# Gate products and branch products of one branch, taken in turn instead of in groups of four

## The chip, the core and the metric

The kernel runs on one core of a Trainium2 chip. The metric is the device time of one execution in microseconds (us), the median of a few runs. TensorE (PE) multiplies matrices, VectorE (DVE) and ScalarE (ACT) do elementwise work, SyncE (SP) issues the large loads.

## What is computed

Two transformer blocks for 256 tokens of width 2048. The part that matters here is the merge of three branches in the first block:

```
p = h @ w_in + b_in
u, v, q, k, v_att, z_pool, gates = jnp.split(p, IN_SPLIT_POINTS, axis=-1)
y_sgu = spatial_gating(...)
y_moba = moba_attention(q, k, v_att)
y_pool = multiscale_pool(...)
g_sgu, g_moba, g_pool = jnp.split(jax.nn.sigmoid(gates), N_BRANCH, axis=-1)
merged = (g_sgu * (y_sgu @ w_sgu_out) + g_moba * (y_moba @ w_moba_out)
          + g_pool * (y_pool @ w_pool_out))
return merged @ w_out
```

Each gate is a product over 2048 input channels, each branch output one over 512. The attention has eight heads, and at 256 tokens each is plain causal attention with a distance term.

## The kernel before

Activations lie with channels on the partitions, so a tile of 128 output channels by 256 tokens is one accumulation in a PSUM bank (`pm`, four banks in rotation). All products are made from two parts of each number, high and low: `mm3` (L363 to L365) issues three matmuls for each 128 input channels. A **gate tile** has 16 such steps, 48 matmuls; a **branch tile** has 4, so 12 matmuls. In the attention, `pd` banks are used.

A weight arrives as one item of 1 MB in a `raw` buffer (load on SP, L222) and is split by `split_piece` in two halves: ScalarE rounds a half to `wh` (L249), VectorE subtracts to get `wl` (L250). There are four `wh` buffers; `wl` and `raw` share nine. One item of `w_in` is the weight of one gate tile; one item of `w_moba_out` serves four branch tiles. Between them items of `w_ada` are mixed in ("sprinkled"), which only VectorE works on (L588, a weighted sum for the modulation).

The program is a list of units. A unit issues its matmuls; then up to four times it advances the pending evictions one step and splits one piece, until the items `ahead` of its own are split. A unit of a branch tile splits at most one piece. The attention (`moba`, L991) is a background generator, moved on one step by each gate unit; whoever needs its result early runs it dry with `until`. Its heads pass scores (VectorE, L1018), exponentials (ScalarE, L1023, L1024), normalisation (VectorE, L1029 to L1031), transposes (TensorE, L1038), a copy (ScalarE, L1040) and products with the values (TensorE, L1049 to L1051); each second head ends with L1055, L411 and L412.

A gate tile is evicted by ScalarE (L850, a tanh). A branch tile is evicted by VectorE (L873), added to the merged tile (L876), and in the last branch split into the two parts that `w_out` reads (ScalarE L414, VectorE L415).

The last branch is `w_moba_out`. Before, its order is: gates 0 to 3, gates 4 to 7, branch tiles 0 to 3, gates 8 to 11, branch tiles 4 to 7, gates 12 to 15, branch tiles 8 to 15. Behind it follows `w_out` with 512-column matmuls (L395 to L397), four items of 24 matmuls for each quarter of the output, beginning with two `pm` banks.

Of the kernel before, what the change touches and what calls it, by code (L numbers as in the profile page):

```python
# [161 lines left out]
class Kernel:  # L162
# [448 lines left out]
    def sprinkle(self, n):  # L611

        self.nada += n
        while self.nada >= 1 and self.more:
            self.nada -= 1
            self.add_item(*self.more.pop(0))
# [212 lines left out]
    def block1_in(self):  # L829
        nc, ins = self.nc, self.ins  # L830
        H = lambda k: self.h[k]
        win = ins["w_in"]
        self.ysgu, self.ymoba, self.ypool = [], [], []
        sprinkle = self.sprinkle

        def tile_unit(idx, fn, pump=1):
            it = self.add_item(win[idx])

            def f(w):
                p = self.psm()  # L840
                for k in range(16):
                    self.mm3(p[:, :T], w, H, k, k == 0, k == 15)
                return fn(p)
            self.unit([it], f, pump=pump)
            sprinkle(self.rate)

        def gate(store, j, bidx):
            def fn(p):
                o = self.hp()[:, :T]
                nc.scalar.activation(o, p[:, :T], AF.Tanh, scale=0.5, bias=self.hb[:, bidx:bidx + 1])  # L850
                store[j] = o
                yield
            return fn


        self.X1 = {}

        def branch(name, ysrc, n4, tg, place):
            it = self.add_item(ins[name][n4])
            for jj in range(4):  # L860
                def f(w, jj=jj):
                    p = self.psm()
                    self.until(lambda: len(ysrc()) == 4)
                    for k in range(4):
                        self.mm3(p[:, :T], w, lambda k: ysrc()[k], k, k == 0, k == 3,
                                 cols=slice(jj * 128, jj * 128 + 128))
                    return ev(n4 * 4 + jj, p)

                def ev(n, p):
                    while tg[n] is None:  # L870
                        yield
                    t = tg[n]
                    nc.vector.scalar_tensor_tensor(t, t, 1.0, p[:, :T], op0=OP.add, op1=OP.mult)  # L873
                    yield
                    if place:
                        nc.vector.tensor_tensor(self.mg[n], self.mg[n], t, op=OP.add)  # L876
                    if place == 2:
                        yield from self.later(2)
                        xt = self.act_tile()
                        self.split_act(xt, self.mg[n], 0.5)  # L880
                        self.X1[n] = xt
                self.unit([it], f, pump=0.4, bg=False, pieces=1)
            sprinkle((0.2, 0.6, 0.4)[place])

        tm, tp = [None] * 16, [None] * 16

        def gates(store, base, n4, pump=1):
            for n in range(n4 * 4, n4 * 4 + 4):
                tile_unit(base + n, gate(store, n, 40 + base + n), pump)
        self.rate = 0.7  # L890
        gates(tp, 16, 0, 2)
        for n4 in range(4):
            if n4 == 2:
                gates(tp, 16, 1)
            branch("w_sgu_out", lambda: self.ysgu, n4, self.mg, 0)
        self.rate = 1
        for n4 in range(4):
            branch("w_pool_out", lambda: self.ypool, n4, tp, 1)
            if n4 < 2:
                gates(tp, 16, n4 + 2)  # L900
        gates(tm, 0, 0)
        for n4 in range(4):
            if n4 < 3:
                gates(tm, 0, n4 + 1)
            branch("w_moba_out", lambda: self.ymoba, n4, tm, 2)

    def sgu(self):
        nc, ins = self.nc, self.ins
# [1231 lines left out]
```

## Time and profile before

| | before |
|---|---|
| median of 3 runs | 2968.15 us (2967.96 to 2971.61) |
| the profiled execution | 2971.89 us, span 2969.8 us |
| granted TensorE clock, mean | 0.994 |
| TensorE matmul busy | 2913.5 us (98%) |
| VectorE busy | 2028.6 us (68%) |
| ScalarE busy | 1418.5 us (48%) |

A busy share is an average over the span; the stretch of the last branch runs from about 430 to 566 us. In a timeline row stand the start in us, the length in us, the engine, the line, the operation with its tiles, and in brackets the idle time of the engine just before, with what ended it. Matmuls overlap, so the distance of two starts tells the pace, not the length of one. The names of tiles are the program's: `wh` and `wl` weights, `act` split activations, `pt` the merged tiles, `hp` small tiles.

### The profile page before, as it was taken

How to read it: one execution, taken by the hardware profiler on the slowest of the kernel's cores; microseconds unless marked ns; L12 is line 12 of the kernel's file. 1: busy time of each engine (PE TensorE's matmuls, PEld its weight loads, DVE VectorE, ACT ScalarE, POOL GpSimd, SP SyncE). 2: the span in 40 equal slices, each digit the busy share in tenths (PEclk: the TensorE clock that was granted, in tenths of full speed). 3: DMA queues.
4: the chain of work that ended last, by engine and by line, in shares of the span. 5: the costliest groups of instructions: out<-in, count | busy, mean ns of one | idle time of the engine just before them, and what ended most of it. 6: DMA issues, size and time to landing. Idle time of an engine off the chain costs nothing.

```text
span 2969.8 us, 44949 instructions
## 1 busy us (share of the span) xinstructions
PE 2913.5 (98%) x18143; PEld 2591.5 (87%) x18143; DVE 2028.6 (68%) x3400; ACT 1418.5 (48%) x2282; POOL 56.9 (2%) x109
## 2 busy tenths in 40 slices
PE   6999999999999999999999999999999999999998
PEld 4999999878888888888899997799988888888887
DVE  7888888878779889676648845555645555555555
ACT  4545444456545556455444344444445444344344
POOL 0000000000000001000000000000000000000000
PEclk9999999999999999999999999999999999999999
DMA  9987778775567677656466773356645555555553
GB/s 360 350 310 279 271 290 335 294 271 175 205 244 263 217 283 258 209 184 213 166 214 199 235 234 107 115 171 242 224 165 184 184 193 187 188 186 183 198 181 131
DMA packets 127233, 660.58 MB, mean 222 GB/s; under 512 B 23009, under 2 KB 36065, under 8 KB 57393
## 3 DMA queue, kind: packets, MB, share of 16 engines
q1 hardware_dynamic: 86258, 603.30, 57.2%
q10 hardware_dynamic: 34464, 35.47, 3.7%
q0 software_dynamic: 6304, 18.95, 1.7%
q8 instruction: 143, 2.34, 0.3%
q14 instruction: 64, 0.52, 0.1%
HBM read 632.42 MB, written 25.23 MB: 221 GB/s over the span
## 4 chain that ended last, share of the span: by engine, by line
PE 90%; DVE 6%; ACT 2%; DMA 1%; issue 1%; SPq 0%; ACTq 0%; DVEq 0%
PE pm L377 22%; PE pm L379 11%; PE pm L363 9%; PE pm L364 9%; PE pm L365 9%; PE pm L395 8%; PE pm L397 8%; PE pm L396 8%; DVE wl L250 3%; ACT wh L249 1%; PE pd L1834 0%; DVE raw L588 0%; PE pd L1770 0%; DMA raw<-w_ada 0%; PE pd L509 0%
## 5 line engine op out<-in xcount | busy, mean ns | idle before, releaser
L250 DVE TENSOR_TENSOR wl<-raw,wh 128x1024 fp32r<-128x1024 f32 (+1 forms) x972 | 1134.7, 1196 | 403.4 <-ACT wh L249 401.1
L249 ACT ACTIVATE wh<-raw 128x1024 fp32r<-128x1024 f32 (+1 forms) x972 | 964.7, 1031 | 317.0 <-PE pm L396 116.9
L377 PE MATMUL pm<-act,wh 128*128 128x512 f32 x2816 | 992.9, 396 | 4.9 <-DVE act L781 3.0
L379 PE MATMUL pm<-act,wl 128*128 128x256 f32 x2816 | 792.0, 281 | 0.0
L363 PE MATMUL pm<-act,wh 128*128 128x256 f32 (+1 forms) x2656 | 756.5, 285 | 5.7 <-DVE hp L873 3.5
L364 PE MATMUL pm<-act,wh 128*128 128x256 f32 (+1 forms) x2656 | 753.2, 284 | 0.9 <-DVE act L781 0.3
L365 PE MATMUL pm<-act,wl 128*128 128x256 f32 (+1 forms) x2656 | 751.0, 283 | 1.7 <-DVE wl L250 1.7
L377 PEld LDWEIGHTS pm<-act,wh 128*128 128x128 f32 x2816 | 529.1, 188 | 127.3 <-DVE act L542 2.3
L379 PEld LDWEIGHTS pm<-act,wl 128*128 128x128 f32 x2816 | 531.5, 189 | 1.2 <-issue 0.7
L363 PEld LDWEIGHTS pm<-act,wh 128*128 128x128 f32 x2656 | 504.9, 190 | 14.3 <-DVE hp L873 4.6
L364 PEld LDWEIGHTS pm<-act,wh 128*128 128x128 f32 x2656 | 503.9, 190 | 2.4 <-DVE act L781 0.7
L365 PEld LDWEIGHTS pm<-act,wl 128*128 128x128 f32 x2656 | 502.0, 189 | 2.3 <-DVE wl L250 2.3
L395 PE MATMUL pm<-wh,act 128*128 128x512 f32 (+1 forms) x1072 | 428.4, 400 | 9.2 <-ACT act L779 5.9
L397 PE MATMUL pm<-wl,act 128*128 128x512 f32 (+1 forms) x1072 | 424.2, 396 | 0.0
L396 PE MATMUL pm<-wh,act 128*128 128x512 f32 (+1 forms) x1072 | 423.2, 395 | 0.5 <-DVE act L781 0.5
L395 PEld LDWEIGHTS pm<-wh,act 128*128 128x128 f32 (+1 forms) x1072 | 201.3, 188 | 60.7 <-ACT act L779 6.5
L396 PEld LDWEIGHTS pm<-wh,act 128*128 128x128 f32 (+1 forms) x1072 | 201.8, 188 | 49.4 <-DVE act L781 1.5
L397 PEld LDWEIGHTS pm<-wl,act 128*128 128x128 f32 (+1 forms) x1072 | 201.5, 188 | 48.9 <-DVE wl L250 0.4
L383 ACT ACTIVATE hp<-pm 128x256 f32<-128x256 f32 x176 | 67.2, 383 | 351.5 <-PE pm L379 351.1
L588 DVE SCALAR_TENSOR_TENSOR raw<-raw,cond 128x2048 f32<-128x2048 f32 x96 | 218.9, 2284 | 5.2 <-DMA raw<-w_ada 5.2
L384 DVE TENSOR_TENSOR hp<-hp,pm 128x256 f32<-128x256 f32 x176 | 73.5, 419 | 210.2 <-ACT hp L383 210.2
L2080 DVE TENSOR_TENSOR x<-pm,x 128x512 f32<-128x512 f32 x32 | 22.1, 692 | 91.7 <-PE pm L397 91.6
(333 smaller groups left out, 1737.2 us busy)
## 6 DMA issues: line engine op xcount, KB each, us to landing
raw<-w_ada SPq DMA_DIRECT2D x96, 1024.0 KB, 6.5
raw<-w_up SPq DMA_DIRECT2D x88, 1024.0 KB, 4.9
raw<-w_ff SPq DMA_DIRECT2D x88, 1024.0 KB, 4.8
raw<-w_in SPq DMA_DIRECT2D x81, 1024.0 KB, 5.1
raw<-w_st SPq DMA_DIRECT2D x37, 1024.0 KB, 6.3
raw<-w_out SPq DMA_DIRECT2D x32, 1024.0 KB, 5.4
raw<-w_down SPq DMA_DIRECT2D x32, 1024.0 KB, 4.9
raw<-w_fd SPq DMA_DIRECT2D x32, 1024.0 KB, 4.8
```

The costliest lines, as they stand in the source:

```text
L249: nc.scalar.activation(vh[:, ks], r[:, ks], AF.Copy)
L250: nc.vector.tensor_tensor(vl[:, ks], r[:, ks], vh[:, ks], op=OP.subtract)
L363: nc.tensor.matmul(o, wh[:, kw, c], x[:, 0, sl], start=start, stop=False, skip_group_check=True)
L364: nc.tensor.matmul(o, wh[:, kw, c], x[:, 1, sl], start=False, stop=False, skip_group_check=True)
L365: nc.tensor.matmul(o, wl[:, kw, c], x[:, 0, sl], start=False, stop=stop, skip_group_check=True)
L377: nc.tensor.matmul(p.rearrange("p (a t) -> p a t", a=2), wh[:, kw, c], x, start=start, stop=False, skip_group_check=True)
L379: nc.tensor.matmul(p[:, T:], wl[:, kw, c], x[:, 0], start=False, stop=stop, skip_group_check=True)
L384: self.nc.vector.tensor_tensor(o, o, p[:, :T], op=OP.add)
L395: nc.tensor.matmul(o, x[:, 0, tok], wh[:, kw], start=start, stop=False, skip_group_check=True)
L396: nc.tensor.matmul(o, x[:, 1, tok], wh[:, kw], start=False, stop=False, skip_group_check=True)
L397: nc.tensor.matmul(o, x[:, 0, tok], wl[:, kw], start=False, stop=stop, skip_group_check=True)
L588: self.nc.vector.scalar_tensor_tensor(o, o, 0.5, self.cond, op0=OP.mult, op1=OP.mult, accum_out=self.m(seg, n))
```

## The change

The last branch gets a helper `one(n)`, called after branch tile n, which puts gate tile n + 2 there. Gates 0 and 1 come first; then branch tile 0, gate 2, branch tile 1, gate 3 and so on to gate 15; branch tiles 14 and 15 are the last. For these units the number of items split ahead is two instead of three. The other two branches stay as they were.

```
-        def tile_unit(idx, fn, pump=1):
+        def tile_unit(idx, fn, pump=1, ahead=3):
...
-            self.unit([it], f, pump=pump)
+            self.unit([it], f, pump=pump, ahead=ahead)
...
-        def branch(name, ysrc, n4, tg, place):
+        def branch(name, ysrc, n4, tg, place, between=None):
...
-                self.unit([it], f, pump=0.4, bg=False, pieces=1)
+                self.unit([it], f, ahead=3 if between is None else 2, pump=0.4, bg=False, pieces=1)
+                if between is not None:
+                    between(n4 * 4 + jj)
...
-        gates(tm, 0, 0)
+        def one(n):
+            if n + 2 < 16:
+                tile_unit(n + 2, gate(tm, n + 2, 42 + n), ahead=2)
+        one(-2)
+        one(-1)
         for n4 in range(4):
-            if n4 < 3:
-                gates(tm, 0, n4 + 1)
-            branch("w_moba_out", lambda: self.ymoba, n4, tm, 2)
+            branch("w_moba_out", lambda: self.ymoba, n4, tm, 2, one)
```

The new code is five lines longer, so a line L991 of before is L996 after, and L1040 is L1045.

On TensorE, behind the second gate tile of this branch, there stood before the products of head 5, the transposes of head 6 (`pg572`), and then the third gate tile (`pm604`):

```order
L1049 MATMUL pd580_4524<-pg582_4532,pt74_350 64x128
L1050 MATMUL pd580_4524<-pg582_4532,pt74_350 64x128
L1051 MATMUL pd580_4524<-pg582_4532,pt75_351 64x128
L1038 MATMUL pd602_4712<-ident_71,pg572_4477 128x128 x3
L363 MATMUL pm604_4721<-act40_195,wh578_4519 128x256
L364 MATMUL pm604_4721<-act40_195,wh578_4519 128x256
L365 MATMUL pm604_4721<-act40_195,wl579_4520 128x256
```

Now the products of head 6 (`pg598` is the copy of its transposes), the transposes of head 7 (`pg588`) and its products follow at once, and then branch tile 0 (`pm599`):

```order
L1054 MATMUL pd580_4524<-pg582_4532,pt74_350 64x128
L1055 MATMUL pd580_4524<-pg582_4532,pt74_350 64x128
L1056 MATMUL pd580_4524<-pg582_4532,pt75_351 64x128
L1043 MATMUL pd597_4698<-ident_71,pg572_4477 128x128 x3
L1054 MATMUL pd600_4708<-pg598_4702,pt74_350 64x128
L1055 MATMUL pd600_4708<-pg598_4702,pt74_350 64x128
L1056 MATMUL pd600_4708<-pg598_4702,pt75_351 64x128
L1043 MATMUL pd601_4712<-ident_71,pg588_4623 128x128 x3
L1054 MATMUL pd600_4708<-pg602_4716,pt74_350 64x128
L1055 MATMUL pd600_4708<-pg602_4716,pt74_350 64x128
L1056 MATMUL pd600_4708<-pg602_4716,pt75_351 64x128
L363 MATMUL pm599_4707<-act529_4154,wh578_4519 128x256
```

The third gate tile, which stood between the heads, has moved behind branch tile 0.

On ScalarE, in the same branch, the evictions of gates 2 to 4 (`pm604`, `pm610`, `pm619`) and the splits between them stood before like this; `wh608` and `wh614` are the weights of gates 5 and 6:

```order
L850 ACTIVATE hp605_4770<-pm604_4721,hb_78 128x256
L249 ACTIVATE wh608_4777<-raw597_4696 128x1024 x2
L850 ACTIVATE hp611_4832<-pm610_4783,hb_78 128x256
L249 ACTIVATE wh614_4839<-raw607_4775 128x1024 x2
L1040 ACTIVATE pg618_4853<-pd617_4849 128x384
L850 ACTIVATE hp620_4904<-pm619_4855,hb_78 128x256
```

Now, at gates 8 to 10 (`pm662`, `pm670`, `pm678`): `wh666` is the branch weight of branch tiles 8 to 11, `wh673` the weight of gate 10 and `wh681` that of gate 11; L414 belongs to branch tiles:

```order
L850 ACTIVATE hp663_5294<-pm662_5245,hb_78 128x256
L249 ACTIVATE wh666_5301<-raw657_5219 128x1024 x2
L414 ACTIVATE act669_5322<-pt137_759 128x256
L850 ACTIVATE hp671_5374<-pm670_5325,hb_78 128x256
L249 ACTIVATE wh673_5378<-raw664_5296 128x1024 x2
L414 ACTIVATE act677_5402<-pt164_969 128x256
L850 ACTIVATE hp679_5454<-pm678_5405,hb_78 128x256
L249 ACTIVATE wh681_5458<-raw672_5376 128x1024 x2
```

The split of a gate's weight stood three gates before its use and now, at these places, stands behind the eviction of the gate just before.

On VectorE, the end of the branch stood before as evictions of neighbouring branch tiles (`pm715`, `pm718`, `pm723`) with pieces of `w_out` weights between them:

```order
L873 SCALAR_TENSOR_TENSOR hp658_5243<-hp658_5243,pm715_5767 128x256
L588 SCALAR_TENSOR_TENSOR raw711_5756,mod_74<-raw711_5756,cond10_97 128x2048
L876 TENSOR_TENSOR pt164_969<-pt164_969,hp658_5243 128x256
L415 SCALAR_TENSOR_TENSOR act717_5785<-pt164_969,act717_5785 128x256
L873 SCALAR_TENSOR_TENSOR hp664_5305<-hp664_5305,pm718_5788 128x256
L250 TENSOR_TENSOR wl721_5805<-raw712_5759,wh720_5804 128x1024
L876 TENSOR_TENSOR pt164_969<-pt164_969,hp664_5305 128x256
L415 SCALAR_TENSOR_TENSOR act722_5809<-pt164_969,act722_5809 128x256
L873 SCALAR_TENSOR_TENSOR hp670_5367<-hp670_5367,pm723_5812 128x256
```

Now the evictions of branch tiles 11 and 12 (`pm703`, `pm710`) have the splits for gates 14 and 15 (`wl709`, `wl717`) between them:

```order
L873 SCALAR_TENSOR_TENSOR hp690_5540<-hp690_5540,pm703_5635 128x256
L876 TENSOR_TENSOR pt165_970<-pt165_970,hp690_5540 128x256
L415 SCALAR_TENSOR_TENSOR act704_5650<-pt165_970,act704_5650 128x256
L250 TENSOR_TENSOR wl709_5707<-raw699_5624,wh708_5706 128x1024 x2
L873 SCALAR_TENSOR_TENSOR hp698_5622<-hp698_5622,pm710_5712 128x256
L588 SCALAR_TENSOR_TENSOR raw700_5627,mod_74<-raw700_5627,cond10_97 128x2048
L876 TENSOR_TENSOR pt170_1034<-pt170_1034,hp698_5622 128x256
L415 SCALAR_TENSOR_TENSOR act712_5730<-pt170_1034,act712_5730 128x256
L250 TENSOR_TENSOR wl717_5787<-raw707_5704,wh716_5786 128x1024 x2
```

Each eviction of a branch tile has moved to a place where one gate's weight is split before the next eviction.

## Rows read from the trace of the kernel before

**Rows 1.** Stretches: us, busy PE, PEld, DVE, ACT, POOL (count), clock, DMA, GB/s.
```profile
440.00:540.00 100.00, 100.00 (x837) 99.09 (x836) 86.11 (x99) 44.80 (x68) 0.00 (x0) 1.00 0.89 333
540.00:566.00 26.00, 20.48 (x123) 17.75 (x122) 20.16 (x39) 11.29 (x18) 0.00 (x0) 0.93 0.60 218
```

**Rows 2.** Waits of TensorE, 543 to 583 us: total us, times, longest.
```profile
PE pm L363 <- DVE hp L873: 3.5, 3, 1.3
PE pm L395 <- DVE hp L873: 2.0, 1, 2.0
```

**Rows 3.** Timeline of TensorE at the start of `w_out`: start, length, what.
```profile
555.88 0.40 PE L397 MATMUL pm<-wl,act 128*128 128x512 f32 x1
558.24 0.69 PE L395 MATMUL pm<-wh,act 128*128 128x512 f32 x1 [1.97 <-DVE hp L873]
558.73 0.63 PE L396 MATMUL pm<-wh,act 128*128 128x512 f32 x1
...
561.99 0.39 PE L395 MATMUL pm<-wh,act 128*128 128x512 f32 x1
```

**Rows 4.** Stretches around the longest wait, columns as in rows 1.
```profile
550.00:555.00 5.00, 3.14 (x24) 2.94 (x24) 3.81 (x9) 2.09 (x4) 0.00 (x0) 1.00 0.37 126
558.00:562.00 4.00, 3.76 (x10) 2.98 (x11) 2.93 (x6) 1.09 (x3) 0.00 (x0) 0.57 0.37 154
```

**Rows 5.** Timeline of TensorE behind gate 1 of the last branch.
```profile
444.51 0.43 PE L1049 MATMUL pd<-pg,pt 128*64 128x128 f32 x2
...
445.31 0.55 PE L1038 MATMUL pd<-ident,pg 128*128 128x128 f32 x3
445.61 0.36 PE L363 MATMUL pm<-act,wh 128*128 128x256 f32 x1
```

**Rows 6.** Timeline of ScalarE: exponentials to L850, attention output to transposes' copy.
```profile
445.37 0.40 ACT L1023 ACTIVATE pg<-pg,sm 128x128 f32<-128x128 f32 x1 [4.09 <-DVE sm L1022]
...
446.26 0.46 ACT L850 ACTIVATE hp<-pm,hb 128x256 f32<-128x256 f32 x1
...
448.51 0.37 ACT L1055 ACTIVATE hp<-pd 128x256 f32<-128x256 f32 x1
...
449.24 0.47 ACT L1040 ACTIVATE pg<-pd 128x384 f32<-128x384 f32 x1
```

**Rows 7.** Timeline of VectorE: a head's scores, a split, L412 with the normalisation.
```profile
443.94 0.54 DVE L1018 SCALAR_TENSOR_TENSOR pg<-dm,pd 128x384 f32<-128x384 f32 x1
...
445.24 2.28 DVE L588 SCALAR_TENSOR_TENSOR raw<-raw,cond 128x2048 f32<-128x2048 f32 x1
...
447.70 2.36 DVE L250 TENSOR_TENSOR wl<-raw,wh 128x1024 fp32r<-128x1024 f32 x2 [0.17 <-ACT wh L249]
449.98 0.42 DVE L412 TENSOR_TENSOR act<-hp,act 128x256 fp32r<-128x256 f32 x1
...
450.97 2.28 DVE L588 SCALAR_TENSOR_TENSOR raw<-raw,cond 128x2048 f32<-128x2048 f32 x1
```

**Rows 8.** Timelines of ScalarE and VectorE: a gate's eviction and a weight's split.
```profile
482.41 0.47 ACT L850 ACTIVATE hp<-pm,hb 128x256 f32<-128x256 f32 x1 [3.34 <-PE pm L365]
482.78 2.00 ACT L249 ACTIVATE wh<-raw 128x1024 fp32r<-128x1024 f32 x2
...
483.87 2.36 DVE L250 TENSOR_TENSOR wl<-raw,wh 128x1024 fp32r<-128x1024 f32 x2 [1.14 <-ACT wh L249]
```

**Rows 9.** Timeline of VectorE: one branch tile's eviction, first and next instruction.
```profile
495.92 0.41 DVE L873 SCALAR_TENSOR_TENSOR hp<-hp,pm 128x256 f32<-128x256 f32 x1
...
497.62 2.28 DVE L588 SCALAR_TENSOR_TENSOR raw<-raw,cond 128x2048 f32<-128x2048 f32 x1
```

**Rows 10.** Timeline of VectorE: L597 to L601, first and next instruction.
```profile
564.16 0.15 DVE L597 TENSOR_TENSOR mod<-mod,vecs 128x4 f32<-128x4 f32 x1
...
565.34 2.29 DVE L588 SCALAR_TENSOR_TENSOR raw<-raw,cond 128x2048 f32<-128x2048 f32 x1
```

**Rows 11.** The page's groups: busy us, mean ns of one, idle before.
```profile
L365 PE MATMUL pm<-act,wl 128*128 128x256 f32 (+1 forms) x2656 | 751.0, 283 | 1.7 <-DVE wl L250 1.7
```

## The prediction

> **What bounds the kernel now.** I read the busy table by stretches first, then TensorE's waits, then the timelines of TensorE, ScalarE and VectorE around the waits. From 440 to 540 us TensorE is busy the whole 100 us at a granted clock of 1.00: 837 matmuls, so one starts each 0.119 us, a gate tile (48) takes 5.7 us and a branch tile (12) 1.43 us [rows 1]. VectorE is busy 86 of those 100 us, so it has little to spare. From 540 to 566 us TensorE is busy for only 20.48 of 26 us [rows 1]. Its waits there are four, all on line L873 of VectorE, which evicts branch tiles: three of branch matmuls (3.5 us) and one of the first `w_out` item (2.0 us) [rows 2]. Four PSUM banks rotate, so the fifth tile in a row waits until the first is evicted. Counted from one matmul's start to the next, with a small further gap of 0.2 us, the four cost 6.3 us (5.5 us of rows 2, and in each some 0.16 us of the matmul's own drain). Behind the longest (555.88 to 558.24 [rows 3]) the granted clock falls to 0.57 in 558 to 562 us, near the lower level of 1.2 GHz, where it was 1.00 before [rows 4]. The starts from 558.24 to 561.99 span nine matmuls in 3.75 us [rows 3]; nine at 0.23 us would take 2.1, so 1.7 us are lost. **6.3 + 1.7 = 8.0 us is all that this stretch can give back.**
>
> **The change, part by part.** No instruction is added or removed on TensorE, ScalarE or VectorE; the order and the places of the loads change.
>
> *Branch tiles apart.* Between two branch tiles now stands a gate tile of 5.7 us, and an eviction takes 1.7 us (L873, L876, ScalarE's L414, L415; 495.92 to 497.62 [rows 9]). All PSUM waits of rows 2 go, except that the last three branch tiles stand near the end with one gate tile among them, which four banks hold: -8.0 us, the clock's share included. The Trainium skill, page "Perfetto Trace Analysis", section "Optimizing Tensor Performance", says that independent groups of matmuls should rotate through PSUM banks so that the eviction of one overlaps the next group. By that rule alone the change would give those 8.0 us; no sentence below rests on it.
>
> *Attention is asked for earlier.* Branch tile 0 needs all eight heads of the attention, which runs in the background between gate tiles. It now stands after gate 1 instead of gate 7. The order of TensorE shows what that does: the products of heads 5, 6 and 7 follow each other with no gate tile between. I follow it from gate 1's end at 444.5 us [rows 5]. TensorE does head 5's products and head 6's transposes until 445.6. ScalarE must evict gate 1 (0.37), split gate 2's weight (1.9) and pass L1055 and L411 (0.73) before it copies head 6's transposes (0.47) [rows 6, 8]: 444.6 + 3.5 = 448.1, so TensorE idles 2.5 us. Head 6's products take 0.8 us [rows 5], to 448.9. Head 7's scores are early (1.3 us of VectorE, free at 439.5; the two exponentials 0.9 us of ScalarE) [rows 6, 7], but their normalisation stands behind VectorE's half of the same split (from 446.1, 2.28 us) and takes 1.0 us with L412 ahead of it [rows 7]: 449.4, idle 0.5. The copy of head 7's transposes on ScalarE then costs 0.8 us of idling and the last L1055, L411 and L412 some 0.3 us. Sum **+4.1 us**. Before, gate tiles hid all of this: rows 1 show no idle time there.
>
> *Gate weights come later.* Before, a weight was split three items ahead. Now the branch weight holds one of the four `wh` buffers for four tiles, the lead is two, and the next branch weight counts as one of them. The order of ScalarE shows that the split of a gate's weight then stands right behind the eviction (L850) of the gate just before it, for gates 3, 6, 7, 10, 11, 14 and 15. From that gate's last matmul the chain is 0.28 (its own time [rows 11]), 0.37 for L850, 1.09 to VectorE's half and 1.22 for the half that TensorE needs first [rows 8], with three hand-overs of 0.05 us (my estimate from the difference of starts): 3.1 us. TensorE has the last matmul's slot, a branch tile and two matmuls that need only the high part, 15 x 0.119 = 1.8 us. It idles 1.3 us. So for gates 3, 7, 11 and 15; for 10 and 14 the eviction of another branch tile stands ahead on ScalarE (0.3 more). 4 x 1.3 + 2 x 1.6 = **+8.4 us**.
> Gate 6 is worse: from the end of gate 4 VectorE has to do an eviction (1.7), two `w_ada` reductions (L588, 2 x 2.2 [rows 7, 9]), the next branch weight's split (2.28), L873 and L876 of branch tile 3 (0.9); then ScalarE L414 and L850 (0.7), and the split up to the first half (2.3 and a hand-over): 12.4 us. TensorE has branch 3, gate 5, branch 4 and two matmuls: 8.8. **+3.6 us.**
>
> *The first items of `w_out`.* After gate 15 the two last evictions (2 x 1.7) and L597 to L601 (1.2 [rows 10]) stand on VectorE between the two halves of the second `w_out` weight. From the start of the first weight's split: 2.28 + 2.2 + 1.14 + 3.4 + 1.2 + 1.22 = 11.4 us; TensorE has 1.3 us until its third matmul starts, and then 36 matmuls at 0.23 = 8.3: idle 1.8, and 0.6 at the first weight. **+2.4 us.**
>
> *The load queue.* The lead of loads also shrinks, but SP's transfers were issued two gate tiles ahead of the split in my walk through the order; DMA's share was 0.89 in 440 to 540 us [rows 1], and a slower TensorE asks for less per us. I take 0; if one weight lands late, the bound is one more wait like that of gate 6, +3.6 us.
>
> *The clock.* It fell after an idle stretch of 2.1 us [rows 3, 4], and not after those of 1.3 us in 550 to 555 us [rows 4]. The stalls in the attention (2.5 us at once) and at gate 6 (3.6 us) are longer than the first; a fall costs up to 1.7 us. None to two: I take one, weighted for its overlap with idling, **+1.4 us**; bounds 0 and 3.4.
>
> **Sum:** 4.1 + 8.4 + 3.6 + 2.4 + 1.4 = +19.9; minus 8.0: **+11.9 us**. The profiled execution took 2971.89 us, 3.7 us above the median of 2968.15; on the former the sum gives 2983.8, on the median, which I forecast, **2980 us** (+0.4%). What follows this stretch keeps TensorE busy (98% over the span), so the delay is carried to the end one to one. A walk of the same kind through the order of before gives 7.0 us for the four waits where the trace has 6.3, so terms of mine may be a tenth too high.
>
> **Rivals.**
> *Gain, 2960 us.* The PSUM waits go and the weights still come in time. It would need the split of gates 7, 10, 11, 14, 15 to be issued at least 1.3 us sooner against TensorE; above that point each gate costs nothing, and if the attention's 4.1 us were hidden as well, -8.0 is left. For it: VectorE idles 14 of 100 us [rows 1]. Against it: the order puts the split behind an eviction that cannot start before the gate ends, and no idle time of VectorE helps that. 0.06.
> *A wash, about 2970 us.* Hand-overs and halves overlap better than I reckon: gates at 0.6 us each (4.2), attention 3, gate 6 and `w_out` 1.5 each, no fall: +10.2 - 8.0 = +2. Against it: each term has its durations in rows. 0.13.
> *The clock swings, 2992 us.* Each of the seven late gates is followed by a stretch at the lower level: 7 x 1.7 = 11.9 more. Against it: the three waits of branch tiles, 3.5 us together [rows 2], left the granted clock at 1.00 in 550 to 555 us [rows 4]. 0.06. The Trainium skill, page "TensorE: Matmul & The Clock Gate", section "A second HAM failure mode: psum-queue depth-cycling", tells of short idle times between groups of matmuls that let the gate swing between its levels, so that throughput suffers; by it this rival would be the result, and rows 4 show the opposite so far.
> That the order does not change as said is excluded by the order of TensorE.
>
> **How the numbers follow.** The forecast, 0.75, has its own range of 2975 (the terms a tenth lower, no fall, gate 6 at half) to 2986 (two falls, one late load). With the wash 0.13, the gain 0.06 and the swing 0.06, the range 2972 to 2988 leaves out the gain, the swing and the lower half of the wash. Faster or slower by over 0.2% (5.9 us), about what a measurement of this kernel can tell from no change: the forecast lies above 2974.1 but for its lowest end, so slower 0.80, same 0.14, faster 0.06.
>
> **What would show it.** In the profile of the changed kernel: no wait on L873 behind branch tiles; TensorE waiting on ScalarE's copy (L1045, before L1040) and VectorE's L1035 near 446 to 451 us; waits of about 1.0 us on VectorE's L250 at the third matmul of gates 3, 7, 10, 11, 14, 15, spaced 8 us apart in pairs, with a longer one at gate 6; one wait in the second `w_out` item; a granted clock below 1 behind the longest of them. I am wrong if gate tiles start without waits, or if the loads of `w_in` rather than the splits are what they wait for.

## The result, and the profile after

| | before | after |
|---|---|---|
| median | 2968.15 us (5 runs, 2967.96 to 2971.61) | 2984.11 us (5 runs, 2982.72 to 2984.88) |
| the profiled execution | 2971.89 us, span 2969.8 us | 2984.01 us, span 2981.8 us |
| granted TensorE clock, mean | 0.994 | 0.993 |
| TensorE matmul busy | 2913.5 us | 2920.0 us |

The changed kernel is slower: ratio 1.0051, 95% interval 1.0038 to 1.0064. The two profiled executions differ by 12.0 us of span, the medians by 16.0. Before each reading below I name the view.

How much of it lies in the stretch that was edited can be read from two landmarks that both programs have: ScalarE's first eviction of a gate tile (L850), and TensorE's first matmul behind the first L605, two items into `w_out` (L605 is a small product that spreads a row of the modulation, from L597 to L601). First the kernel before, timelines of ScalarE and TensorE (start, length, what):

```profile
282.36 0.46 ACT L850 ACTIVATE hp<-pm,hb 128x256 f32<-128x256 f32 x1
...
570.68 0.79 PE L395 MATMUL pm<-wh,act 128*128 128x512 f32 x1
```

The same two of the changed kernel:

```profile
282.08 0.45 ACT L850 ACTIVATE hp<-pm,hb 128x256 f32<-128x256 f32 x1
...
583.25 0.80 PE L395 MATMUL pm<-wh,act 128*128 128x512 f32 x1
```

From one to the other it takes 288.3 us before and 301.2 after: **+12.9 us, which is the whole difference of the two spans (12.0 us) and 0.9 us more.** Below I call this the length of the stretch.

The changed kernel by stretches, columns as in [rows 1] and the first two windows the same ones:

```profile
440.00:540.00 100.00, 90.58 (x704) 86.78 (x703) 70.45 (x89) 38.80 (x59) 0.00 (x0) 0.97 0.71 265
540.00:566.00 26.00, 24.14 (x197) 23.33 (x196) 21.24 (x24) 8.13 (x12) 0.00 (x0) 1.00 0.84 319
...
450.00:454.00 4.00, 3.80 (x18) 3.47 (x19) 0.42 (x1) 0.95 (x3) 0.00 (x0) 0.57 0.52 221
...
487.00:491.00 4.00, 3.25 (x16) 3.12 (x15) 4.00 (x4) 0.51 (x1) 0.00 (x0) 0.60 0.76 270
...
525.00:565.00 40.00, 37.30 (x302) 36.08 (x302) 31.03 (x36) 15.41 (x22) 0.00 (x0) 1.00 0.79 299
```

Where TensorE was busy for all of 440 to 540 us, it now idles 9.4 of the 100, with 704 matmuls in place of 837. The granted clock falls twice, to near 1.2 GHz, in 450 to 454 and in 487 to 491 us; in 525 to 565 us, with three late gates (11, 14 and 15), it stays at 1.00.

Waits of TensorE in the changed kernel, 425 to 640 us (total us, times, longest):

```profile
PE pm L365 <- DVE wl L250: 5.5, 8, 0.8
PE pd L1054 <- ACT pg L1045: 2.9, 2, 2.3
PE pm L363 <- ACT wh L249: 2.3, 3, 1.8
PE pm L397 <- DVE wl L250: 1.4, 2, 1.1
PE pd L1043 <- DVE pg L1035: 0.3, 1, 0.3
PE pm L395 <- ACT wh L249: 0.2, 1, 0.2
```

The waits on L873 of [rows 2] are gone, all of them. In their place stand waits on the two halves of a weight (L249, L250) and on the attention (L1045, L1035). Of the eight on L365, seven are those of gates 3, 6, 7, 10, 11, 14 and 15, and one is in branch tile 4.

**The attention.** Timeline of TensorE before branch tile 0:

```profile
445.02 0.55 PE L1043 MATMUL pd<-ident,pg 128*128 128x128 f32 x3
447.84 0.43 PE L1054 MATMUL pd<-pg,pt 128*64 128x128 f32 x2 [2.28 <-ACT pg L1045]
...
449.01 0.61 PE L1043 MATMUL pd<-ident,pg 128*128 128x128 f32 x3 [0.31 <-DVE pg L1035]
450.20 0.68 PE L1054 MATMUL pd<-pg,pt 128*64 128x128 f32 x2 [0.58 <-ACT pg L1045]
```

ScalarE in the same place; the copy L1045 that TensorE wants at 445.3 stands last of these rows:

```profile
444.32 0.47 ACT L850 ACTIVATE hp<-pm,hb 128x256 f32<-128x256 f32 x1 [2.73 <-PE pm L365]
444.69 1.99 ACT L249 ACTIVATE wh<-raw 128x1024 fp32r<-128x1024 f32 x2
446.59 0.37 ACT L1060 ACTIVATE hp<-pd 128x256 f32<-128x256 f32 x1
446.99 0.42 ACT L411 ACTIVATE act<-hp 128x256 fp32r<-128x256 f32 x1
447.31 0.47 ACT L1045 ACTIVATE pg<-pd 128x384 f32<-128x384 f32 x1
```

**The late gates.** At gate 6 TensorE waits for the rounded half and then for the other one:

```profile
484.53 0.28 PE L365 MATMUL pm<-act,wl 128*128 128x256 f32 x1
486.62 0.39 PE L363 MATMUL pm<-act,wh 128*128 128x256 f32 x1 [1.81 <-ACT wh L249]
486.84 0.28 PE L364 MATMUL pm<-act,wh 128*128 128x256 f32 x1
487.88 0.58 PE L365 MATMUL pm<-act,wl 128*128 128x256 f32 x1 [0.75 <-DVE wl L250]
```

On ScalarE gate 6's split stands behind gate 5's eviction (485.17), and that behind branch tile 3's L414. VectorE held this up, with two L588 and the next branch weight's split ahead of the tile's L873 and L876:

```profile
484.84 0.42 ACT L414 ACTIVATE act<-pt 128x256 fp32r<-128x256 f32 x1 [5.72 <-DVE pt L876]
```

The cause of the others is plain on ScalarE and VectorE at gate 11. ScalarE:

```profile
526.57 0.47 ACT L850 ACTIVATE hp<-pm,hb 128x256 f32<-128x256 f32 x1 [1.33 <-PE pm L365]
526.94 2.94 ACT L249 ACTIVATE wh<-raw 128x1024 fp32r<-128x1024 f32 x3
```

VectorE, at the same time:

```profile
528.02 2.36 DVE L250 TENSOR_TENSOR wl<-raw,wh 128x1024 fp32r<-128x1024 f32 x2 [2.33 <-ACT wh L249]
```

ScalarE idles 1.33 us for gate 10's last matmul, then evicts, then splits; VectorE idles 2.33 us for the split. Both engines were idle just before, so by these rows it was the order that kept them from doing this weight earlier; the second experiment tests that.

### The profile page after: what moved, and what is told of

Read it like the earlier page. It is cut to its first block, busy times and chain, and to the rows that moved or that the text cites. A ratio compares the mean times of both kernels' runs of the same rounds, so it can differ in the third digit from the quotient of the medians.

```text
span 2981.8 us, 44945 instructions
## 1 busy us (share of the span) xinstructions
PE 2920.0 (98%) x18143; PEld 2594.1 (87%) x18143; DVE 2029.3 (68%) x3400; ACT 1417.5 (48%) x2282; POOL 56.9 (2%) x109
## 4 chain that ended last, share of the span: by engine, by line
PE 88%; DVE 8%; ACT 2%; DMA 1%; issue 1%; ACTq 0%; SPq 0%; DVEq 0%
PE pm L377 22%; PE pm L379 11%; PE pm L363 9%; PE pm L365 9%; PE pm L364 9%; PE pm L397 8%; PE pm L395 8%; PE pm L396 8%; DVE wl L250 3%; DVE raw L588 1%; ACT wh L249 1%; PE pd L1839 0%; PE pd L1775 0%; PE pm L527 0%; DMA raw<-w_ada 0%
## 5 line engine op out<-in xcount | busy, mean ns | idle before, releaser
L250 DVE TENSOR_TENSOR wl<-raw,wh 128x1024 fp32r<-128x1024 f32 (+1 forms) x972 | 1134.8, 1196 | 412.3 <-ACT wh L249 410.1
L249 ACT ACTIVATE wh<-raw 128x1024 fp32r<-128x1024 f32 (+1 forms) x972 | 964.0, 1031 | 325.4 <-PE pm L396 116.5
L377 PE MATMUL pm<-act,wh 128*128 128x512 f32 x2816 | 990.5, 396 | 4.9 <-DVE act L781 3.0
L379 PE MATMUL pm<-act,wl 128*128 128x256 f32 x2816 | 789.9, 281 | 0.0
L365 PE MATMUL pm<-act,wl 128*128 128x256 f32 (+1 forms) x2656 | 753.6, 284 | 6.9 <-DVE wl L250 6.8
L377 PEld LDWEIGHTS pm<-act,wh 128*128 128x128 f32 x2816 | 528.8, 188 | 127.0 <-DVE act L542 2.3
L379 PEld LDWEIGHTS pm<-act,wl 128*128 128x128 f32 x2816 | 531.0, 189 | 1.1 <-issue 0.7
L365 PEld LDWEIGHTS pm<-act,wl 128*128 128x128 f32 x2656 | 504.0, 190 | 9.4 <-DVE wl L250 9.4
L588 DVE SCALAR_TENSOR_TENSOR raw<-raw,cond 128x2048 f32<-128x2048 f32 x96 | 218.8, 2284 | 4.2 <-DMA raw<-w_ada 4.2
```

Of the source, the lines that this page charges most:

```text
L249: nc.scalar.activation(vh[:, ks], r[:, ks], AF.Copy)
L250: nc.vector.tensor_tensor(vl[:, ks], r[:, ks], vh[:, ks], op=OP.subtract)
L365: nc.tensor.matmul(o, wl[:, kw, c], x[:, 0, sl], start=False, stop=stop, skip_group_check=True)
L377: nc.tensor.matmul(p.rearrange("p (a t) -> p a t", a=2), wh[:, kw, c], x, start=start, stop=False, skip_group_check=True)
L379: nc.tensor.matmul(p[:, T:], wl[:, kw, c], x[:, 0], start=False, stop=stop, skip_group_check=True)
L588: self.nc.vector.scalar_tensor_tensor(o, o, 0.5, self.cond, op0=OP.mult, op1=OP.mult, accum_out=self.m(seg, n))
```

## The experiments

All medians are beside runs of the kernel before on the same chip; the 28 of the first group have a median of 2969.06 us. The last column is the length of the stretch in the one profiled execution, less the 288.3 us of before.

| | median us | ratio to before, 95% interval | stretch |
|---|---|---|---|
| after | 2984.11 | 1.0051, 1.0038 to 1.0064 | +12.9 |
| attention sooner | 2974.57 | 1.0017, 1.0008 to 1.0026 | +11.0 |
| pieces first | 2966.51 | 0.9988, 0.9979 to 0.9997 | -3.2 |
| both | 2960.39 | 0.9971, 0.9959 to 0.9982 | -3.9 |
| smaller groups | 2973.00 | 1.0010, 1.0001 to 1.0018 | -1.0 |
| lead of two alone | 2971.45 | 1.0007, 0.9998 to 1.0016 | +4.1 |
| before, attention sooner | 2968.69 | 1.0001, 0.9992 to 1.0010 | +1.0 |
| more banks | 2964.47 | 0.9985, 0.9976 to 0.9994 | -3.0 |
| both, `w_out` first | 2961.36 | 0.9972, 0.9962 to 0.9983 | -4.0 |
| banks, L605 later | 2957.84 | 0.9960, 0.9946 to 0.9974 | -7.3 |

(The two with more banks move L605, or end a fall of the clock behind it; their end landmark is the first matmul behind the second L605, a quarter of `w_out` later, and the length stands against 311.3 us of before.)

### The attention moved on sooner

```
-                gates(tp, 16, n4 + 2)
+                gates(tp, 16, n4 + 2, 2)
```

> The changed kernel, with the gate units of the pool branch ahead of it moving the attention on twice as fast, so that all heads are done before branch tile 0 asks for them. Theory (the attention's tail is asked for too early and costs its own 4.1 us, and about 1.7 us of lost clock behind it): the waits of TensorE on ScalarE's copy (L1045, 2.9 us in the changed kernel) and on VectorE's L1035 (0.3 us) near 446 to 451 us are gone, the granted clock stays at 1.00 there, the waits on L250 and L249 at the gates stay as they are, and the time falls by 4 to 6 us against the changed kernel, to about 2978 to 2980 us. Rival (the attention is short of VectorE or ScalarE time wherever it stands): the waits move some tens of us earlier into the pool branch and the time stays within 1.5 us of the changed kernel, 2982.5 to 2985.5.

Waits of TensorE, 425 to 640 us:

```profile
PE pm L365 <- DVE wl L250: 6.0, 9, 0.8
PE pm L363 <- ACT wh L249: 2.3, 3, 1.8
PE pm L397 <- DVE wl L250: 1.4, 2, 1.1
PE pm L395 <- ACT wh L249: 0.2, 1, 0.2
```

The waits on the attention and the first fall of the clock are gone, as the theory has it, and the rest stays. The median fell by 9.5 us, more than either view expected, but the stretch gave only 1.9 back: gate 2 now waits as well (a ninth wait on L250; the attention's wait had covered it), and the fall at gate 6 lasts twice as long (0.55 in 483 to 487 us, 0.60 in 487 to 491). Of the 3.8 us of waits and 1.7 of clock that went, gate 2 takes 1.2, and the longer fall 1.6 by the granted clock (0.9 by the distances of starts); the 0.8 to 1.5 us that remain were not followed to the end. One wait of 0.4 us on L873, in the pool branch, is new. So the attention's own price is confirmed by the waits that went, but alone it gives back half, because the next late thing stood right behind. The other 7.6 us came from outside the stretch, and their cause is open (see the end).

### The pieces of the next weight ahead of the evictions

```
+            if ahead == 2 and pieces == 4:
+                for s in range(4):
+                    if self.split < goal:
+                        self.split_piece()
+                pieces = 0
             for s in range(stages):
                 self.advance()
```

> The changed kernel, but a gate unit of the last branch issues the pieces of the next weight's split ahead of the eviction steps, so that ScalarE's split does not stand behind the tanh (L850) of the gate just before. Theory (a gate's weight is late by its place in ScalarE's queue, 8.4 us in all and 3.6 at gate 6): the waits on L250 (5.5 us, 8 times) and on L249 (2.3 us, 3 times) behind the gates go or fall under 1 us together, the clock falls once instead of twice, the attention's 3 us stay, and the time falls by 9 to 13 us, to 2971 to 2975 us. Rival (the weights are late because their loads land late, or because VectorE has no time left for the split): the waits stay, or become waits on a DMA, and the time stays within 3 us of the changed kernel, 2981 to 2987.

Five lines are added above the lines named here, so L370 is L365 of before, L1059 is L1049 and L855 is L850. Waits of TensorE, 425 to 640 us:

```profile
PE pd L1059 <- ACT pg L1050: 1.4, 2, 0.8
PE pm L402 <- DVE wl L250: 0.9, 1, 0.9
PE pm L370 <- DVE wl L250: 0.8, 1, 0.8
PE pm L400 <- ACT hp L855: 0.2, 1, 0.2
PE pm L368 <- ACT wh L249: 0.2, 1, 0.2
```

ScalarE at the same gate as above; the split now stands ahead of the eviction:

```profile
512.77 0.42 ACT L419 ACTIVATE act<-pt 128x256 fp32r<-128x256 f32 x1 [4.00 <-DVE pt L881]
513.10 2.94 ACT L249 ACTIVATE wh<-raw 128x1024 fp32r<-128x1024 f32 x3
515.95 0.45 ACT L855 ACTIVATE hp<-pm,hb 128x256 f32<-128x256 f32 x1
```

This decides the main question. With the same loads, the same work on each engine and the same lead of two, the 7.8 us of waits on L250 and L249 become 1.0, the clock does not fall in the stretch, and the time falls by 17.6 us, to just below the kernel before. The rival (loads, or VectorE's time) is out but for gate 6: the 1.0 us are all its own, since its split still stands behind L419 (L414 of before), which waits 5.72 us for VectorE as it did. It gave more than I expected since the attention's copies also stood behind a split (3.2 us of its waits become 1.4, and the fall behind them goes).

### Both edits

> Both edits of the changed kernel together: the attention moved on sooner, and the pieces of the next gate's weight ahead of the eviction steps. Theory (the terms add): only the waits of w_out's first items are left, about 1.5 to 2.5 us, no fall of the clock in 440 to 560 us, and the time is 2965 to 2969 us, at or a little below the kernel before. Rival (with the queues rearranged something that has no wait now becomes late, VectorE's evictions of branch tiles or the loads): the sum of the two single gains is not reached, and the time is over 2972 us.

Only three waits are left, 1.9 us together: 0.8 and 0.9 on L250 (gate 6 and `w_out`'s second item), 0.2 on L855. The time is 2960.39, under the range of the theory; its stretch of -3.9 us is what the theory needs, and more came from outside the stretch (3.4 us by the two profiled spans, 4.8 by the medians). So the order in turn, with its weights in time, is a gain over the groups, of which the stretch shows 3.9 us.

### Smaller groups, and lead of two alone

The kernel before, with eight, four, two and two gates ahead of its four groups of branch tiles:

```
-        gates(tm, 0, 0)
-        for n4 in range(4):
-            if n4 < 3:
-                gates(tm, 0, n4 + 1)
+        for g, n4 in ((8, 0), (4, 1), (2, 2), (2, 3)):
+            for n in range((0, 8, 12, 14)[n4], (0, 8, 12, 14)[n4] + g):
+                tile_unit(n, gate(tm, n, 40 + n))
             branch("w_moba_out", lambda: self.ymoba, n4, tm, 2)
```

> The kernel before, with its lead of three and its groups, but gates 12 to 15 not in one group: gates 0 to 7, branch tiles 0 to 3, gates 8 to 11, branch tiles 4 to 7, gates 12 and 13, branch tiles 8 to 11, gates 14 and 15, branch tiles 12 to 15, so that eight branch tiles never follow each other. Theory (the waits on L873 come from more branch tiles in a row than there are PSUM banks, and the gate weights are in time as long as the lead is three and the branch weight is held for a short time only): the three waits of branch tiles on L873 (3.5 us) are gone, the one at w_out (2.0 us) stays or shrinks, the clock stays at 1.00 if it shrinks, and the time falls by 4 to 8 us against the kernel before, to 2960 to 2964 us. Rival (the time is set by VectorE's work for the evictions and the splits, and the waits only change their names): the time stays within 2 us of 2968, with waits on L250 or at w_out of as many us as those that went.

Waits of TensorE, 425 to 640 us, and the window behind the longest:

```profile
PE pm L395 <- DVE hp L873: 4.1, 2, 3.0
PE pm L363 <- DVE hp L873: 0.6, 1, 0.6
```

```profile
552.00:558.00 6.00, 4.28 (x9) 2.99 (x10) 4.85 (x10) 1.78 (x3) 0.00 (x0) 0.50 0.86 347
```

My theory fell. The branch tiles' waits shrank from 3.5 us to 0.6, but that of `w_out` grew from 2.0 to 4.1 in two, and the clock stood at 0.50 for 6 us with them. The profiled execution was the fastest of eleven, so its stretch of -1.0 us may flatter the edit; the median is 4 us above before. Here a wait for a bank is also a wait for VectorE's queue: the smaller groups ask for the same evictions at the end.

The kernel before, with a lead of two items in place of three for the gates and branch tiles of the last branch, and its order as it was:

```
...
-                self.unit([it], f, pump=0.4, bg=False, pieces=1)
+                self.unit([it], f, ahead=2 if place == 2 else 3, pump=0.4, bg=False, pieces=1)
...
-                tile_unit(base + n, gate(store, n, 40 + base + n), pump)
+                tile_unit(base + n, gate(store, n, 40 + base + n), pump, 3 if base else 2)
```

Waits of TensorE, 425 to 640 us:

> The kernel before, with its groups, and only the other half of the change: the lead of the splits is two items instead of three for the gates and the branch tiles of the last branch. Theory (a lead of two is long enough as long as gate tiles stand in groups, since a gate tile is 5.7 us and a split 2.3; the weights come late only where an item that serves four tiles is interleaved and the split falls behind the eviction of the gate just before): no wait on L250 or L249 over 1 us in all, the waits on L873 as before, and the time within 3 us of the kernel before, 2966 to 2972 us. Rival (the lead alone makes the weights late): waits on L250 or L249 behind the gates of 5 to 12 us in all, and 2974 to 2984 us.

```profile
PE pm L363 <- DVE hp L873: 3.5, 3, 1.3
PE pm L395 <- DVE hp L873: 2.8, 1, 2.8
PE pm L365 <- DVE wl L250: 2.7, 2, 1.3
```

Between the two views: the lead alone makes two weights late, one behind each of two branch groups (2.7 us where I allowed 1, under the rival's 5 to 12), and `w_out` waits 0.8 us longer. The stretch grew by 4.1 us, the median by 2.4, which its interval cannot tell from nothing. Interleaving with a lead of three was not run; by my reading of the code the branch weight would hold one of the four `wh` buffers while ScalarE's next split waits for a buffer that is freed only behind it.

### The kernel before with the attention sooner

The edit of the first experiment on the kernel before.

> The kernel before, with the gate units of the pool branch moving the attention on twice as fast, as in the first experiment; nothing waited for the attention here. In that experiment the stretch of the last branch gave some 2 us back, and 7.5 us were gained far behind it, where the pairs of matmuls of L377 and L379 between 2300 and 2900 us started every 348.0 ns instead of 350.8. Theory (this far gain belongs to the earlier attention, by the places at which later tiles lie, and not to the waits of the last branch): the waits on L873 stay, the pairs start every 348 ns, and the time is 2963 to 2967 us. Rival (it was a chance of single executions, or it needs the interleaved order): the pairs keep 350.8 ns and the time stays within 2 us of 2969.

The waits on L873 are as they were and the median is unchanged, so the earlier attention is worth nothing by itself. The pairs of matmuls came every 349.6 ns, about half-way; the theory of the far gain is not borne out.

### More banks

```
-                    p = self.psm()
+                    p = self.pss() if place == 2 and jj % 2 else self.psm()
```

> The kernel before, order and lead as they were, but every second branch tile of the last branch takes its PSUM bank from pd instead of pm, so that eight tiles in a row find a bank free. Theory (the waits on L873 are for a PSUM bank and nothing else): the three waits of branch tiles (3.5 us) and the one of w_out (2.0 us) go, the granted clock stays at 1.00, and 8.0 us are given back: 2960 to 2963 us. Rival (VectorE is behind with the evictions and the splits, as the group of four smaller groups suggests, whose wait at w_out grew to 4.1 us): the same idle time comes back in w_out's first items, as waits on L873, on L415 or on L250 of together 4 to 7 us, and the time stays within 3 us of 2969.

Waits of TensorE, 425 to 640 us:

```profile
PE pd L605 <- DVE ad L601: 3.5, 1, 3.5
```

The instruction on VectorE that it waited for, which stands behind the last eviction:

```profile
564.44 0.87 DVE L601 TENSOR_SCALAR ad<-ident,mod 128x128 f32<-128x128 f32 x4
```

Both views hold in part. All four waits on L873 go with nothing but other banks, so it was the banks; and 3.5 us of idle time come back at the first instruction that needs VectorE to be through, with a fall of the clock behind it (0.64 in 565.4 to 569.4 us). 4.6 of 8.0 us are left.

### More banks, and L605 later

The edit above, and this one:

```
-        for _ in range(6):
+        for _ in range(18 if seg == 2 and q == 0 else 6):
             yield
         p = self.pss()
```

> The kernel with more banks, and one more edit: the matmul L605 of w_out's first quarter, which waited 3.5 us for L601 because VectorE still had eight evictions and splits ahead of it, is issued twelve steps of its unit later, in the next item. Theory (the 8.0 us of the PSUM waits are all there, and the kernel with more banks gave half back only because L605 was next in TensorE's queue): the wait on L601 goes, its fall of the clock goes too (1.7 us), a wait of about 1 us on L250 may come in w_out's fourth item, and the time falls by 4 to 5 us to 2959.5 to 2961 us, level with the interleaved order with both edits. Rival (VectorE is that far behind for every reader, so the idle time only moves to the next one): waits on L415 or L250 of 3 us or more in w_out's third and fourth items, and the time stays at 2963 to 2966 us.

Waits of TensorE, 425 to 640 us, and the stretch of [rows 1] in which it idled 5.5 us before:

```profile
PE pm L397 <- DVE wl L250: 0.8, 1, 0.8
```

```profile
540.00:566.00 26.00, 26.00 (x161) 23.34 (x161) 20.03 (x41) 11.13 (x17) 0.00 (x0) 1.00 0.74 280
```

The theory holds: one wait of 0.8 us is left, the clock stays at 1.00, and the stretch is 7.3 us shorter than before. At 2957.84 us this is the lowest median of all, without any change of the order of gates and branch tiles; its interval overlaps that of the kernel with both edits, but its stretch is 3.4 us shorter.

### Both edits, and w_out's weights first

In the kernel with both edits, the last two branch tiles may split up to four pieces ahead of their evictions.

```
-                self.unit([it], f, ahead=3 if between is None else 2, pump=0.4, bg=False, pieces=1)
+                self.unit([it], f, ahead=3 if between is None else 2, pump=0.4, bg=False,
+                          pieces=4 if between is not None and n4 * 4 + jj > 13 else 1)
```

> The kernel with both edits (attention sooner, split pieces ahead of the evictions in gate units), and the last two branch tiles too issue the pieces of w_out's weights ahead of their evictions, up to four pieces instead of one. Theory (the second w_out weight is late because its second half stands behind the two last evictions and L597 to L601): the wait on L250 in w_out's second item (0.9 us, 1.1 by starts) is gone, and the time is 2958 to 2960 us, 1 to 2 us under the kernel with both edits. Rival (the evictions that now stand later are what w_out needs next): a wait of 1 to 3 us on L420 or L878 in w_out's third or fourth item takes its place, 2960 to 2963 us.

Neither view, for the edit changed nothing that ran: from 440 to 600 us ScalarE and VectorE have the same instructions in the same order as without it. By the code, the goal of these two units counts two items from the branch weight, and those are the weights of gates 14 and 15, which are split by then. So the wait on L250 stays at 0.9 us, 2961.36 us is a second measurement of the kernel with both edits, and the theory was not tested. The second half still stands behind the two evictions and L602 to L606 (L597 to L601 of before).

## Why the prediction held, point by point

*The sum.* Forecast +11.9 us on the profile; the spans differ by 12.0. The terms, forecast and measured. A measured term is the sum of the distances of two starts in TensorE's timeline, less the usual slot (0.12 us for 256 columns, 0.23 for 512, 0.30 for the three transposes):

| term | forecast | measured |
|---|---|---|
| PSUM waits and their fall | -8.0 | -8.0 (no wait on L873 is left; the price is that of before) |
| attention | +4.1 | +3.8 (2.5, 0.4, 0.9) |
| gates 3, 7, 11, 15 | +5.2 | +4.6 (4 x 1.16) |
| gates 10, 14 | +3.2 | +2.7 (2 x 1.33) |
| gate 6 | +3.6 | +3.2 (2.9, and 0.3 at branch tile 4) |
| first items of `w_out` | +2.4 | +2.1 (0.50, 0.38, 1.26) |
| falls of the clock | +1.4 | +3.3 (0.43 x 4, 0.40 x 4) |
| load queue | 0 | 0 (no wait on a load) |
| sum | +11.9 | +11.7 |

The stretch is 12.9 us longer; 1.2 us lie in gaps too small to name. Each term of waiting was about a tenth too high, as the walk through the kernel before had said of itself: together 18.5 forecast, 16.4 measured. The term that failed is **the clock**: two falls, where I took one. They came where I had put them, behind the attention's stall and behind gate 6, and the reason that I gave (idle stretches longer than the 2.1 us one of [rows 3]) would, with the 2.5 and 3.6 us forecast there, have given both; I cut them to one, and that by 0.3, for overlap with idling. Gate 6's stall then came as 2.0 and 0.9 us with two matmuls between, so it was not one longer stretch, and the clock fell all the same. The window from 487 us shows an overlap with idling, but of 0.75 us only. The two errors, 2.1 us too high in the waits and 1.9 too low in the clock, nearly cancel; that the sum came out within 0.3 us is in part luck.

*The mechanism.* The second experiment shows it: a gate's weight is late by its place behind the eviction of the gate before in ScalarE's order. At gate 6 VectorE's two L588 come on top, as forecast; waits of 0.2 and 0.8 us are left there under the edit. The first shows that the attention stalled because it was asked for early.

*The rivals.* The gain at 2960 was put at 0.06, and on the order as it is that was right; its condition, a split issued at least 1.3 us sooner, is what the experiment with both edits gave, and the time came out as 2960.4; about half of that gain lies outside the stretch, though. The wash needed late gates of 0.6 us each; they took 1.16 and 1.33. The swing of the clock did not come: with three late gates in 525 to 565 us the granted clock stayed at 1.00. The Trainium skill, page "TensorE: Matmul & The Clock Gate", section "A second HAM failure mode: psum-queue depth-cycling", tells of a kernel whose short idle times between groups of matmuls made the clock swing. Here waits of 1.2 to 1.3 us, in pairs some 8 us apart, did not.

*The -8.0 us.* It was right as a term of this change, since branch tiles now stand apart, but "all that this stretch can give back" needed a second condition, which the prediction did not name: VectorE must be through by the next instruction that reads from it. With more banks alone 4.6 us came back, with L605 moved as well 11.1 in the median and 7.3 in the stretch. The Trainium skill's advice to rotate banks (page "Perfetto Trace Analysis", section "Optimizing Tensor Performance") is borne out by these two runs, once that reader is out of the way.

*The base.* I put the sum on the median of before; after's median came out 4 us higher. The profiled execution of before was one of its slower ones: among the 28 of the first group, the eleven with a granted clock of 0.993 or 0.994 took 2971.2 us in the mean, the seventeen with 0.995 or 0.996 took 2968.6. The five runs of after lie within 2.2 us, all at 0.992 or 0.993. Two falls in the stretch against one explain part of that. Why none of the five was as lucky elsewhere as most runs of before is open.

## What to carry to other kernels

In these traces ScalarE and VectorE took their instructions in the order of the program: ScalarE idled 1.33 us with gate 11's split next behind an eviction. So how many items ahead a weight is prepared counted less than which instruction stood before it. When tiles are interleaved, look for the preparation that now stands behind an eviction that cannot start before TensorE ends the tile in front; issuing it ahead of that eviction was worth 17.6 us here. And before reordering for a PSUM wait, see whether another bank is free: here two one-line edits gave the lowest median, with the order left alone.

## What the runs showed that I had not expected

Far behind the edit, TensorE's pace differs between these programs. Windows of 2300 to 2900 us, columns as in [rows 1], TensorE busy throughout; first the kernel before, then the one with the attention sooner:

```profile
2300.00:2900.00 600.00, 600.00 (x3170) 513.73 (x3169) 323.56 (x392) 262.49 (x368) 0.00 (x0) 1.00 0.54 187
```

```profile
2300.00:2900.00 600.00, 600.00 (x3193) 515.49 (x3192) 326.74 (x397) 265.01 (x373) 0.00 (x0) 1.00 0.54 189
```

0.7% more matmuls in the same time at the same clock: 4 us. In the one trace of each kernel, a pair of L377 and L379 takes 350.8 ns in before, after and pieces first, 348.0 in attention sooner, in both edits and in both with `w_out` first, 348.4 in banks with L605 later, and 349.2 to 350.4 in the rest. No instruction of that part was edited. The cause is open: the one experiment on it (before, attention sooner) was inconclusive. It means that of a difference of 4 us between two programs here, nothing should be put down to an edit unless the stretch of the edit shows it.
